# Row-wise infinity norm: two block sizes for the bulk rows and two stores instead of one

## The chip, the cores and the metric

The kernel runs on one core of a Trainium2 chip. The metric is the device time of one execution in microseconds (us); lower is better. Before the change three runs gave 626.51, 626.56 and 626.67 us, median 626.56.

## The reference

```python
x = np.random.randn(8192, 8192).astype(np.float32)   # 268 MB
out = np.linalg.norm(x, ord=np.inf, axis=1)           # per row
...
```

With `ord=np.inf` and `axis=1`, each row is a vector and its norm is the largest absolute value in it. So 8192 rows of 8192 floats (32 KB a row) are each reduced to one float. All of x has to be read once; the output is 32 KB.

## The kernel before, in words

The 8192 rows are spread over the 128 partitions, 64 rows to each. They come in two parts.

**Bulk.** The first 48 rows of each partition's share are read in A = 4 blocks. In one block, a partition owns G x B = 6 x 2 = 12 adjacent rows of HBM, so the places that two neighbouring partitions read from lie 12 rows (384 KB) apart. A block is read in six loads (line 303) of two rows a partition: 64 KB into each of the 128 partitions, 8.39 MB a load. After each load VectorE reduces it with one instruction, called at line 304 and recorded at line 296, to the absolute maximum of both rows, and writes two columns of the tile `r_bulk`. There are 24 such loads and 24 such reductions.

**Tail.** The last 16 rows of each partition's share are adjacent in HBM (512 KB from partition to partition). They are read in eight tiles of two rows as well, but each tile is cut into several loads of falling width (`TAIL`, lines 315 to 319, and `LAST`, lines 337 to 350), so that VectorE can start on each piece early. The partial maxima go to the tile `part`, or, for the last tile, beside its own data; the results go to `r_tail`. The narrow reductions of the last tile are the ones written `t<-t` in the profile.

**Queues and order.** All loads are issued by SP. There are three buffers `t`; a load into one waits until VectorE has reduced what was in it, so that SP is mostly two loads ahead of VectorE. The counters of DMA completion are used in turn; each is called a lane, DMAHW0 to DMAHW7 in the program's listing. ACT issues one store, that of `r_bulk` (line 357), ordered behind the last reduction but two of the last tile. The store of `r_tail` (line 359) is issued by SP after the last reduction. Five rewrites of the finished program (lines 360 to 364) then move the first load ahead of the opening barrier, drop waits that others imply, and let POOL close the program: it waits for the other open counters, clears the two ranges of counters on either side of the last store's lane, and finally waits for that last store (`finish_on_pool`).

Of the kernel before, what the change touches and what calls it, by code (L numbers as in the profile page):

```python
# [12 lines left out]
F32 = mybir.dt.float32  # L13
# [17 lines left out]
    + [(1, w) for w in (1664, 1408, 1280, 1152, 1024, 896)]  # L31
    + [(0, 768), (1, 768)]
)


HEAD, STEP = 32, 8


def segments(loads, cols):

    out, at = [], 0
    for i, w in enumerate(loads):
        end = at + w
        while at < end:
            r = at // cols
            to = min(end, (r + 1) * cols)
            out.append((i, r, at - r * cols, to - at))
            at = to
    return out
# [201 lines left out]
@with_exitstack  # L251
def kernel(
    ctx: ExitStack,
    tc: tile.TileContext,
    x: bass.AP,
    out: bass.AP,
    G: int = 6,
    B: int = 2,
    BUFS: int = 3,
    PAD: int = 256,  # L260
    LINE: int = 128,
):
    nc = tc.nc
    P = nc.NUM_PARTITIONS
    rows, cols = x.shape
    W = B * cols


    n_tail = B * (len(TAIL) + 1)
    n_bulk_rows = rows // P - n_tail  # L270
    assert n_bulk_rows % (G * B) == 0
    A = n_bulk_rows // (G * B)
    split = n_bulk_rows * P
    x_b = x[:split].rearrange("(a p n b) c -> a n p (b c)", p=P, a=A, n=G, b=B)
    out_b = out[:split].rearrange("(a p n b) -> p a (n b)", p=P, a=A, n=G, b=B)
    x_t = x[split:].rearrange("(p t b) c -> t p (b c)", p=P, b=B)
    out_t = out[split:].rearrange("(p t) -> p t", p=P)

    outp = ctx.enter_context(tc.tile_pool(name="outp", bufs=1))
    sbuf = ctx.enter_context(tc.tile_pool(name="sbuf", bufs=BUFS))  # L280

    segs = [segments(loads, cols) for loads in TAIL]
    k_max = max(sum(r == b for _, r, _, _ in s) for s in segs for b in range(B))
    parts_of = [sum(r == b for r, _ in LAST) - 1 for b in range(B)]
    assert sum(parts_of) <= PAD

    r_bulk = outp.tile([P, A, G * B], F32)
    r_tail = outp.tile([P, n_tail], F32)
    part = outp.tile([P, n_tail - B, k_max], F32)
    used = [HEAD, A * G * B, n_tail, (n_tail - B) * k_max]  # L290
    gap = -sum(-(-n // STEP) * STEP for n in used) % LINE
    outp.tile([P, gap], F32, name="gap")
    nc.gpsimd.memset(part[:], 0.0)  # L293

    def absmax(o, i):
        return nc.vector.reduce_max(  # L296
            out=o, in_=i, axis=X, apply_absolute_value=True
        )

    for a in range(A):  # L300
        for n in range(G):
            t = sbuf.tile([P, W + PAD], F32, tag="t")
            nc.sync.dma_start(out=t[:, :W], in_=x_b[a, n])
            absmax(
                r_bulk[:, a, n * B : (n + 1) * B],
                t[:, :W].rearrange("p (b c) -> p b c", b=B),
            )

    for i, loads in enumerate(TAIL):
        t = sbuf.tile([P, W + PAD], F32, tag="t")  # L310
        todo = segs[i]
        seen = [0] * B
        at = 0
        for j, w in enumerate(loads):
            nc.sync.dma_start(out=t[:, at : at + w], in_=x_t[i][:, at : at + w])
            at += w
            for _, b, c, n in [s for s in todo if s[0] == j]:
                k, lo = seen[b], b * cols + c
                absmax(part[:, i * B + b, k : k + 1], t[:, lo : lo + n])
                seen[b] += 1  # L320

    def after(ins, first, kind):
        info = mybir.DependencyInfo(kind, mybir.DependencyReason.SCHED_ONLY)
        tc.add_manual_dep(ins.ins, first.ins.name, info, reason="order")


    t = sbuf.tile([P, W + PAD], F32, tag="t")
    left = parts_of[:]
    col = [0] * B
    at, slot = 0, {}  # L330
    ends = [w for _, w in LAST[-B:]]
    lo = W - sum(ends)
    for b in range(B):
        slot[b] = -(-lo // LINE) * LINE + ends[b]
        lo = slot[b] + parts_of[b]
    assert lo <= W + PAD
    for j, (b, w) in enumerate(LAST):
        final = left[b] == 0
        to = slot[b] - w if final else at
        frm = b * cols + col[b]  # L340
        nc.sync.dma_start(out=t[:, to : to + w], in_=x_t[len(TAIL)][:, frm : frm + w])
        col[b] += w
        if final:
            r = n_tail - B + b
            absmax(r_tail[:, r : r + 1], t[:, to : slot[b] + parts_of[b]])
        else:
            left[b] -= 1
            k = slot[b] + left[b]
            done = absmax(t[:, k : k + 1], t[:, to : to + w])
            at += w  # L350
        if j == 0:

            ins = absmax(r_tail[:, : n_tail - B], part[:])
            after(ins, done, mybir.DependencyClass.NoSync)
        if j == len(LAST) - 3:

            ins = nc.scalar.dma_start(out=out_b, in_=r_bulk[:])
            after(ins, done, mybir.DependencyClass.Sync)
    nc.sync.dma_start(out=out_t, in_=r_tail[:])
    nc.at_finalize(clear_partials_early)  # L360
    nc.at_finalize(drop_implied_waits)
    nc.at_finalize(start_first_load_early)
    nc.at_finalize(finish_on_pool)
    nc.at_finalize(open_without_vector)
# [30 lines left out]
```

## Time and profile before

| What | Value |
|---|---|
| Median of three runs | 626.56 us |
| Span of the profiled execution (first to last recorded instruction) | 624.1 us |
| Time around the span, 626.56 - 624.1 | 2.5 us |
| DMA engines, mean rate over the span | 430 GB/s |
| One bulk load from issue to landing, median | 40.7 us |
| Bulk, first to last landing (21.76 to 466.68 us) | 444.92 us |
| Tail, last bulk landing to the start of the last pair of reductions | 154.79 us |
| Store of `r_bulk` from issue to landing | 2.4 us |
| Store of `r_tail` from issue to landing | 1.4 us |

The profiled execution is known by its span; its total time is not recorded apart from it, so the runs' median stands beside it. A line of instruction groups reads: line of the code, engine, operation, output and input tile with shapes, count, then the busy time in us, the mean of one in ns, and the idle time of the engine ahead of them with what ended it. A DMA issue's own length is the time that the issuing engine was occupied; the transfer goes on behind it until it lands. q1 is the queue of SP, q10 that of ACT.

### The profile page before, as it was taken

How to read it: one execution, taken by the hardware profiler on the slowest of the kernel's cores; microseconds unless marked ns; L12 is line 12 of the kernel's file. 1: busy time of each engine (PE TensorE's matmuls, PEld its weight loads, DVE VectorE, ACT ScalarE, POOL GpSimd, SP SyncE). 2: the span in 40 equal slices, each digit the busy share in tenths (PEclk: the TensorE clock that was granted, in tenths of full speed). 3: DMA queues.
4: the chain of work that ended last, by engine and by line, in shares of the span. 5: the costliest groups of instructions: out<-in, count | busy, mean ns of one | idle time of the engine just before them, and what ended most of it. 6: DMA issues, size and time to landing. Idle time of an engine off the chain costs nothing.

```text
span 624.1 us, 151 instructions
## 1 busy us (share of the span) xinstructions
DVE 552.4 (89%) x63; POOL 0.3 (0%) x5
## 2 busy tenths in 40 slices
DVE  0688988889988899888898888988889999999999
POOL 0000000000000000000000000000000000000000
DMA  9999999999999999999999999999999999999998
GB/s 403 470 403 454 420 428 445 403 470 403 470 403 441 433 403 470 403 470 403 470 403 470 403 462 412 437 437 403 470 434 397 440 448 422 422 437 430 429 427 354
DMA packets 8593, 268.47 MB, mean 430 GB/s; under 512 B 1424, under 2 KB 1424, under 8 KB 2832
## 3 DMA queue, kind: packets, MB, share of 16 engines
q1 hardware_dynamic: 8064, 268.44, 99.7%
q10 hardware_dynamic: 528, 0.02, 0.1%
q14 instruction: 1, 0.01, 0.0%
HBM read 268.44 MB, written 0.03 MB: 430 GB/s over the span
## 4 chain that ended last, share of the span: by engine, by line
DMA 63%; DVE 36%; another core or an unknown queue 0%; DVEq 0%; issue 0%
DMA t<-in_x_dram 63%; DVE r_bulk L296 25%; DVE part L296 8%; DVE t L296 3%; DVEq L390 0%; DVE r_tail L296 0%
## 5 line engine op out<-in xcount | busy, mean ns | idle before, releaser
L296 DVE TENSOR_REDUCE r_bulk<-t 128x2 f32<-128x16384 f32 x24 | 413.3, 17220 | 70.6 <-DMA t<-in_x_dram 70.6
L296 DVE TENSOR_REDUCE part<-t 128x1 f32<-128x8192 f32 (+19 forms) x26 | 121.3, 4741 | 0.3
L296 DVE TENSOR_REDUCE t<-t 128x1 f32<-128x1792 f32 (+7 forms) x10 | 16.3, 1692 | 0.0
L296 DVE TENSOR_REDUCE r_tail<-t 128x1 f32<-128x772 f32 (+1 forms) x2 | 1.8, 948 | 0.0
L296 DVE TENSOR_REDUCE r_tail<-part 128x14 f32<-128x42 f32 x1 | 0.2, 192 | 0.0
L293 POOL MEMSET part<- 128x42 f32 x1 | 0.1, 133 | 0.0
L379 POOL MEMSET const-bfloat16-1.0<- 128x1 bf16 x1 | 0.1, 101 | 0.0
L379 POOL MEMSET const-uint8-127<- 128x1 uint8 x1 | 0.1, 101 | 0.0
L379 POOL MEMSET const-float32-0.0<- 128x1 f32 x1 | 0.1, 98 | 0.2 <-issue 0.2
L379 POOL MEMSET const-float32-1.0<- 128x1 f32 x1 | 0.1, 98 | 0.0
## 6 DMA issues: line engine op xcount, KB each, us to landing
t<-in_x_dram SPq DMA_DIRECT2D x2, 4672.0 KB, 37.5
t<-in_x_dram SPq DMA_DIRECT2D x2, 3520.0 KB, 36.2
t<-in_x_dram SPq DMA_DIRECT2D x1, 6336.0 KB, 36.3
t<-in_x_dram SPq DMA_DIRECT2D x1, 5696.0 KB, 40.5
t<-in_x_dram SPq DMA_DIRECT2D x2, 1792.0 KB, 34.3
t<-in_x_dram SPq DMA_DIRECT2D x1, 3392.0 KB, 37.5
t<-in_x_dram SPq DMA_DIRECT2D x1, 3008.0 KB, 44.2
t<-in_x_dram SPq DMA_DIRECT2D x1, 2496.0 KB, 27.3
```

The lines of the kernel that those rows point to most:

```text
L293: nc.gpsimd.memset(part[:], 0.0)
L296: return nc.vector.reduce_max(out=o, in_=i, axis=X, apply_absolute_value=True)
L379: nc = _bacc.Bacc("TRN2", target_bir_lowering=False, num_devices=1)
```

## The change

The bulk's 48 rows a partition come no longer as four blocks of 12 adjacent rows, but as four blocks of 6 and then one block of 24. Each load still takes two adjacent rows from each partition's place, so there are 4 x 3 + 1 x 12 = 24 loads of the same size, and 24 reductions of the same shape, into the same columns. The result tile has 48 columns as before. Two neighbouring partitions' places lie 6 rows (192 KB) apart in the first four blocks and 24 rows (768 KB) in the last one.

As the two kinds of block leave their rows in two different patterns in the output, `r_bulk` is stored by two DMAs on ACT, one after the other, instead of one: 128 x 4 pieces of 6 floats (24 bytes), and 128 pieces of 24 floats (96 bytes). Before it was one of 128 x 4 pieces of 12 floats (48 bytes). The second store takes the next lane, DMAHW1, and waits for that lane's earlier load; the closing on POOL has one more counter to wait for.

```diff
+BLOCKS = [(4, 3), (1, 12)]
...
-    A = n_bulk_rows // (G * B)
-    split = n_bulk_rows * P
-    x_b = x[:split].rearrange("(a p n b) c -> a n p (b c)", p=P, a=A, n=G, b=B)
-    out_b = out[:split].rearrange("(a p n b) -> p a (n b)", p=P, a=A, n=G, b=B)
+    bulk, lo = [], 0
+    for a, g in BLOCKS:
+        hi = lo + a * g * B * P
+        bulk.append(
+            (
+                a,
+                g,
+                lo // P,
+                x[lo:hi].rearrange("(a p n b) c -> a n p (b c)", p=P, a=a, n=g, b=B),
+                out[lo:hi].rearrange("(a p m) -> p a m", p=P, a=a),
+            )
+        )
+        lo = hi
...
-    r_bulk = outp.tile([P, A, G * B], F32)
+    r_bulk = outp.tile([P, n_bulk], F32)
...
-    for a in range(A):
-        for n in range(G):
-            t = sbuf.tile([P, W + PAD], F32, tag="t")
-            nc.sync.dma_start(out=t[:, :W], in_=x_b[a, n])
-            absmax(
-                r_bulk[:, a, n * B : (n + 1) * B],
-                t[:, :W].rearrange("p (b c) -> p b c", b=B),
-            )
+    for a, g, col, x_b, _ in bulk:
+        for i in range(a):
+            for n in range(g):
+                t = sbuf.tile([P, W + PAD], F32, tag="t")
+                nc.sync.dma_start(out=t[:, :W], in_=x_b[i, n])
+                absmax(
+                    r_bulk[:, col : col + B],
+                    t[:, :W].rearrange("p (b c) -> p b c", b=B),
+                )
+                col += B
...
-            ins = nc.scalar.dma_start(out=out_b, in_=r_bulk[:])
-            after(ins, done, mybir.DependencyClass.Sync)
+            for a, g, c, _, out_b in bulk:
+                r = r_bulk[:, c : c + a * g * B]
+                ins = nc.scalar.dma_start(
+                    out=out_b, in_=r.rearrange("p (a m) -> p a m", a=a)
+                )
+                after(ins, done, mybir.DependencyClass.Sync)
```

More of the change, by code (lines that the diff above doesn't have):

```diff
@@ L256 @@
     out: bass.AP,
-    G: int = 6,
     B: int = 2,
@@ L269 @@
     n_tail = B * (len(TAIL) + 1)
-    n_bulk_rows = rows // P - n_tail
-    assert n_bulk_rows % (G * B) == 0
-    A = n_bulk_rows // (G * B)
-    split = n_bulk_rows * P
-    x_b = x[:split].rearrange("(a p n b) c -> a n p (b c)", p=P, a=A, n=G, b=B)
-    out_b = out[:split].rearrange("(a p n b) -> p a (n b)", p=P, a=A, n=G, b=B)
+    n_bulk = rows // P - n_tail
+    assert n_bulk == sum(a * g * B for a, g in BLOCKS)
+    split = n_bulk * P
+    bulk, lo = [], 0
[11 more added lines that the diff above has]
+        lo = hi
     x_t = x[split:].rearrange("(p t b) c -> t p (b c)", p=P, b=B)
@@ L285 @@
     assert sum(parts_of) <= PAD
-    r_bulk = outp.tile([P, A, G * B], F32)
+    r_bulk = outp.tile([P, n_bulk], F32)
     r_tail = outp.tile([P, n_tail], F32)
     part = outp.tile([P, n_tail - B, k_max], F32)
-    used = [HEAD, A * G * B, n_tail, (n_tail - B) * k_max]
+    used = [HEAD, n_bulk, n_tail, (n_tail - B) * k_max]
     gap = -sum(-(-n // STEP) * STEP for n in used) % LINE
```

## The prediction

> **What bounds the kernel now.** I read the page first, then the groups of instructions, the stretches, the timeline of VectorE and the DMA queues of the last microseconds. The page's busy shares and queue shares:
>
> ```profile
> DVE 552.4 (89%) x63; POOL 0.3 (0%) x5
> ...
> q1 hardware_dynamic: 8064, 268.44, 99.7%
> q10 hardware_dynamic: 528, 0.02, 0.1%
> ```
>
> The 16 DMA engines work on SP's loads (q1) for 99.7% of the span; VectorE, at 89%, has room. The groups say where that room is:
>
> ```profile
> L296 DVE TENSOR_REDUCE r_bulk<-t 128x2 f32<-128x16384 f32 x24 | 413.3, 17220 | 70.6 <-DMA t<-in_x_dram 70.6
> L296 DVE TENSOR_REDUCE part<-t 128x1 f32<-128x8192 f32 (+19 forms) x26 | 121.3, 4741 | 0.3
> ```
>
> All of VectorE's idle time of any size (70.6 us) stands before the 24 bulk reductions, and each time it ends with a load. So the bulk, the only part whose addresses the change touches, is bound by its loads. How evenly they come is seen in VectorE's timeline, where each start marks a landing (start, length, what, idle before it):
>
> ```profile
> 137.84 17.22 DVE L296 TENSOR_REDUCE r_bulk<-t 128x2 f32<-128x16384 f32 x1 [2.21 <-DMA t<-in_x_dram]
> 157.34 17.22 DVE L296 TENSOR_REDUCE r_bulk<-t 128x2 f32<-128x16384 f32 x1 [2.29 <-DMA t<-in_x_dram]
> ...
> 331.43 17.22 DVE L296 TENSOR_REDUCE r_bulk<-t 128x2 f32<-128x16384 f32 x1 [2.08 <-DMA t<-in_x_dram]
> 350.71 17.22 DVE L296 TENSOR_REDUCE r_bulk<-t 128x2 f32<-128x16384 f32 x1 [2.06 <-DMA t<-in_x_dram]
> ```
>
> The slowest gap between two landings is 157.34 - 137.84 = 19.50 us, the fastest 350.71 - 331.43 = 19.28 us. The stretches give the rate of the stages (stretch, length, VectorE, POOL, clock, DMA share, GB/s): the whole bulk from its first landing to its last, the tail, then those two gaps.
>
> ```profile
> 21.76:466.68 444.92, 396.05 (x23) 0.00 (x0) 1.00 1.00 433
> 466.68:621.47 154.79, 154.53 (x38) 0.00 (x0) 1.00 1.00 428
> 137.84:157.34 19.50, 17.22 (x1) 0.00 (x0) 1.00 1.00 430
> 331.43:350.71 19.28, 17.22 (x1) 0.00 (x0) 1.00 1.00 435
> ```
>
> The mean gap of the bulk is 444.92 / 23 = 19.34 us, 0.06 above the fastest one. In the tail DMA and VectorE are both full.
>
> **The time that the sum is made against.** The profiled execution is given by its span, 624.1 us; the runs' median is 626.56, so 2.5 us lie around the span. At least 0.6 of these come after it: the last store is issued at 623.31 and lands 1.4 us later, at 624.7. I assume the same 2.5 us after the change.
>
> **Part 1: the bulk's addresses.** Instructions, tiles, DMAs, waits and their order are the same on SP and VectorE: 24 loads of 128 x 16384 floats, still two adjacent rows (64 KB) from each partition's place, into the same buffers; 24 reductions of 17.22 us. What changes is the distance between partitions in HBM: 12 rows of 32 KB = 384 KB before, and now 6 rows = 192 KB for 24 rows a partition (12 loads) and 24 rows = 768 KB for the other 24 (12 loads). Nothing is added or removed, so only a different rate of the loads can pay or cost.
>
> What it can gain: if all 23 gaps became as short as the fastest, 444.92 - 23 x 19.28 = 1.5 us. No gap that is shorter stands in this trace, and the slow ones stand together: between the landings at 118.41 and 196.16 us four gaps in a row are 19.40 to 19.50, all of them in the second block, while the third and fourth blocks have gaps of 19.28 to 19.37 at the very same spacing. So the unevenness does not go by the spacing, and I expect none of the 1.5 us from it.
>
> What it can cost: the nearest rows are 384 KB (19.34 us a load) and the tail, whose partitions lie 16 rows = 512 KB apart: 155.6 us from the last bulk landing at 466.66 to the start of the last reduction at about 622.3, 8 x 8.39 MB, or 19.45 us for as much as one bulk load, with 32 smaller DMAs instead of 8. That is 0.11 more, and it includes the smaller sizes. If the 12 loads at 768 KB took that, it were 12 x 0.11 = 1.3 us. By the slowest gap, 0.16 above the mean, 12 loads cost 1.9 us and 24 cost 3.8. VectorE hides none of this: it idles 2.1 us a load and starts each reduction at the landing. I take zero, as 384 KB and the power of two 512 KB both stream with the DMA share at 1.00, and 768 is twice, 192 half of the spacing that the whole bulk has now.
>
> The Trainium skill speaks against such a change in "DMA: Bandwidth & Descriptors", section "Latency and other measured facts": copies whose rows lie large powers of two apart slow down, from 207 GB/s at 512 KiB to 164 at 2 MiB. The tail at 512 KB here agrees with the harmless end (428 GB/s); 192 and 768 KB are no powers of two and lie below 2 MiB, so by the rule as written I would add nothing, and no run here yet shows 768 KB. If 768 KB behaved as its 2 MiB row, an estimate from that page would be 12 x 19.3 x (207/164 - 1) = 61 us.
>
> **Part 2: one store becomes two.** The old bulk store moves 512 pieces of 48 bytes; now ACT issues one of 512 pieces of 24 bytes and a second of 128 pieces of 96. The end of the profile:
>
> ```profile
> 621.47 1.81 DVE L296 TENSOR_REDUCE r_tail<-t 128x1 f32<-128x772 f32 x2
> 621.59 0.41 ACTq L357 DMA_DIRECT2D out_dram<-r_bulk  x1
> 623.31 0.35 SPq L359 DMA_DIRECT2D out_dram<-r_tail  x1
> ```
> ```profile
> out_dram<-r_bulk ACTq DMA_DIRECT2D x1, 24.0 KB, 2.4
> out_dram<-r_tail SPq DMA_DIRECT2D x1, 8.0 KB, 1.4
> ```
>
> The second issue comes after the first, at 621.59 + 0.41 = 622.0, and takes 0.35 (r_tail's row) to 0.41, so ACT is free at about 622.4. Nothing is queued behind it but the end of the program, and that waits anyway for SP, which issues its last store at 623.31 to 623.66. The second store also waits for the lane (completion counter) DMAHW1 that it reuses: the load of 1408 columns, which landed before its reduction (1.61 us); the next one (1.48 us) ended where the last three before `r_tail` begin, at 618.10, so that load is some 5 us old by 621.59 and the wait costs nothing.
>
> Landing: the old store lands at 621.59 + 2.4 = 624.0. The second store's lower bound is r_tail's 1.4 us after its issue, 623.4; the upper bound is another 2.4, 624.4, if it queues fully behind the first. The queue's packets bear out less: q10 took 25.6% of 16 engines over 1.3 us for 528 packets, that is 0.256 x 1.3 x 16 / 528 = 0.010 us each. The 144 further packets (128 and 16 completions) are 9 an engine, 0.09 us. I take 624.1 for both. The cover is r_tail's store, which lands at 624.7: 0.6 us of room, 0.3 at the upper bound. From 623.2 to 624.1 no queue moves a packet in the trace, so the bulk store's packets are through 0.9 us before r_tail's begin, and 0.09 us more of them should not meet those.
>
> POOL closes the program after the other stores' counters and then r_tail's; one more wait is added, for the second bulk store. What POOL does between them isn't in the trace. If that work fills all the time after 624.0, a later bulk landing moves the end one for one: 0.1 us by my value, 0.4 at the upper bound. In the other direction two shorter stores could land earlier than one, but as r_tail's 624.7 stays, that gains at most a few hundredths.
>
> **Sum:** loads 0, reductions 0, stores 0 to 0.1: span 624.1, time 626.6 us.
>
> **The rivals.**
> - A, the stores come to the front: the second one lands at 624.4 and POOL's closing work is what ends last. 626.56 + 0.4 = 627.0. For it: two stores in one ring, and an unseen closing. Against it: 0.09 us by the packets. Still within 0.2%. It decides once the landing plus POOL's work passes 624.7.
> - B, slower: the block with 768 KB spacing streams less evenly in HBM, as in the slow gaps of this trace. At 0.16 us a load, 12 loads give 1.9 us: 628.5; if both new spacings do, 630.4. For it: gaps up to 19.50 exist, so something slows single loads. Against it: two different spacings run at full DMA share. It passes 0.2% (1.25 us) once each of the 12 loads takes 0.10 us more.
> - C, faster: the slow gaps were the old spacing's doing and all loads come at 19.28: 626.56 - 1.5 = 625.1. Against it: two of the four equal blocks already run without them.
> - D, the change doesn't do what it says: only addresses and one store differ, so there is nothing that a scheduler could undo; no chance of its own.
>
> **How the numbers follow.** Forecast 626.6 with 0.62; A 0.20; B 0.13; C 0.05. Forecast and A lie within 0.2%, which is about what a measurement of this kernel can tell from no change. Of C some 0.04 passes that bound, the full 1.5 us being needed nearly whole; of B some 0.12. So faster 0.04, same 0.84, slower 0.12. The range goes from 625.8 (half of C's gain) to 627.6 (A, and 0.05 us on each of 12 loads); B in full and C in full are left out.
>
> **What would show it.** Right: gaps between bulk landings of 19.3 us in both kinds of block, bulk stretch near 445 us; two ACT issues from 621.6 to 622.5; the second store landing before 624.7. B shows as gaps over 19.4 in the last 12 bulk loads alone, C as gaps of 19.28 all through, A as an unchanged span with a longer time, since POOL's close lies behind the span. I am wrong if the DMA share stays at 1.00 while a bulk stretch drops below 430 GB/s.

## The result and the profile after

The changed kernel takes 627.77 us (median of 20 runs, 627.39 to 628.16), the kernel before 626.57 (20 runs, 626.28 to 626.83): ratio 1.0019, 95% interval 1.0013 to 1.0026. It is slower by 1.2 us, just outside the range given. The profiled execution took 627.82 us, but its span is 624.0 us, no longer than the 624.1 of before. So 3.8 us lie around the span, where the table above has 2.5 for before. That 2.5 sets the runs' median against the span of another execution; taken within one execution, time minus span is 2.58 to 2.73 us in all 148 executions of the kernel before that were run beside the experiments (median 2.63), and 3.55 to 4.00 in the 20 of the changed kernel (median 3.82). So all of the 1.2 us lies around the span.

The page of the changed kernel shows the queues and VectorE as they were; q10 alone, the stores' queue, has 144 packets more:

```profile
DVE 552.4 (89%) x63; POOL 0.3 (0%) x5
...
q1 hardware_dynamic: 8064, 268.44, 99.7%
q10 hardware_dynamic: 672, 0.02, 0.1%
...
L308 DVE TENSOR_REDUCE r_bulk<-t 128x2 f32<-128x16384 f32 x24 | 413.3, 17220 | 70.6 <-DMA t<-in_x_dram 70.6
L308 DVE TENSOR_REDUCE part<-t 128x1 f32<-128x8192 f32 (+19 forms) x26 | 121.3, 4741 | 0.3
```

VectorE's idle time is 70.6 us again, all of it before the bulk's reductions. The timeline of VectorE in the changed kernel, at its longest and at one of its shortest gaps between landings:

```profile
234.67 17.22 DVE L308 TENSOR_REDUCE r_bulk<-t 128x2 f32<-128x16384 f32 x1 [2.15 <-DMA t<-in_x_dram]
254.13 17.22 DVE L308 TENSOR_REDUCE r_bulk<-t 128x2 f32<-128x16384 f32 x1 [2.24 <-DMA t<-in_x_dram]
...
331.39 17.22 DVE L308 TENSOR_REDUCE r_bulk<-t 128x2 f32<-128x16384 f32 x1 [2.08 <-DMA t<-in_x_dram]
350.67 17.22 DVE L308 TENSOR_REDUCE r_bulk<-t 128x2 f32<-128x16384 f32 x1 [2.06 <-DMA t<-in_x_dram]
```

The longest gap is 19.46 us, between the two kinds of block; that pair apart, the 192 KB loads take (234.67 - 22.03) / 11 = 19.33 us each, and the 768 KB loads (466.64 - 254.13) / 11 = 19.32. The stretches of the changed kernel (bulk from first to last landing, then the tail; columns as before) say the same:

```profile
22.03:466.64 444.61, 396.06 (x23) 0.00 (x0) 1.00 1.00 433
466.64:621.43 154.79, 154.53 (x38) 0.00 (x0) 1.00 1.00 428
```

444.61 us against 444.92, and the tail equal. The loss is in none of this. Now the end of the changed kernel, in its timeline and in its DMA issues (size of one in KB, median us from issue to landing):

```profile
621.43 1.81 DVE L308 TENSOR_REDUCE r_tail<-t 128x1 f32<-128x772 f32 x2
621.55 0.97 ACTq L373 DMA_DIRECT2D out_dram<-r_bulk  x2
623.27 0.35 SPq L377 DMA_DIRECT2D out_dram<-r_tail  x1
```
```profile
out_dram<-r_bulk ACTq DMA_DIRECT2D x2, 12.0 KB, 3.7
out_dram<-r_tail SPq DMA_DIRECT2D x1, 8.0 KB, 2.5
```

The issues come when they did before; the landings do not. The store of `r_tail`, unchanged and issued at 623.27, lands 2.5 us after its issue instead of 1.4: at 625.8 instead of 624.7, 1.1 us late. The tile's view of the output in the changed kernel has the three times to landing (3.9 is that of the first bulk store):

```profile
L373 ACTq DMA_DIRECT2D out_dram<-r_bulk x2: 412/464/517, 621.5 to 622.0; - x2
L377 SPq DMA_DIRECT2D out_dram<-r_tail x1: 348/348/348, 623.3 to 623.3; - x1
...
DMA to landing us min/median/max: 2.5/3.6/3.9
```

Read with the issue times, the bulk stores land 3.9 us after 621.55 and 3.6 after 622.00: at about 625.4 and 625.6, just ahead of `r_tail`'s 625.8. Were they still moving data? The DMA queues from 621.9 to 623.2 (40 slices of 0.03 us, then packets), before and then after:

```profile
DMA  0000000000000000080057998788768621110000
...
q10 hardware_dynamic: 528, 0.02, 25.6%
```
```profile
DMA  0000000000000000061356776677731011147553
...
q10 hardware_dynamic: 667, 0.02, 26.0%
```

Before, the last packets of the bulk store run at about 623.1, and it lands 0.9 us later, at 624.0. In the changed kernel 667 of q10's 672 packets start before 623.2, and the remaining five right behind, so the bulk stores' packets were through 2.2 us before the first landing. `r_tail`'s own packets are as early as before; the queues from 623.5 to 625.5 (slices of 0.05 us), before and then after:

```profile
DMA  0000000000000465200000000000000000000000
DMA  0000000000002653000000000000000000000000
```

They end near 624.4 both times, and `r_tail` lands 0.3 us later before and 1.4 us later after. What is late is not the transfer of either store but what comes between the last packet and the landing.

From that landing the end follows at a nearly fixed distance in every profiled run of this study, 1.9 to 2.0 us: 627.82 - 625.8 here; 626.57 (the median) - 624.7 before; 1.9 to 2.0 in all 18 experiments, each by the time of its profiled execution. So the time is the landing of the last store plus 2.0; what POOL does behind that landing takes the same time in every run.

### The profile page after: what moved, and what is told of

The parts are those of the page before. It is cut to its first block, busy times and chain, and to the rows that moved or that the text cites. A ratio compares the mean times of both kernels' runs of the same rounds, so it can differ in the third digit from the quotient of the medians.

```text
span 624.0 us, 152 instructions
## 1 busy us (share of the span) xinstructions
DVE 552.4 (89%) x63; POOL 0.3 (0%) x5
## 4 chain that ended last, share of the span: by engine, by line
DMA 63%; DVE 36%; another core or an unknown queue 0%; DVEq 0%; issue 0%
DMA t<-in_x_dram 63%; DVE r_bulk L308 25%; DVE part L308 8%; DVE t L308 3%; DVEq L408 0%; DVE r_tail L308 0%
## 5 line engine op out<-in xcount | busy, mean ns | idle before, releaser
L308 DVE TENSOR_REDUCE r_bulk<-t 128x2 f32<-128x16384 f32 x24 | 413.3, 17220 | 70.6 <-DMA t<-in_x_dram 70.6
```

The lines of the kernel that those rows point to most:

```text
L308: return nc.vector.reduce_max(out=o, in_=i, axis=X, apply_absolute_value=True)
```

## The experiments

Theory S: the bulk stores' completion is late, and the last store's waits behind it. Rival L blames the loads, rival N the mere second store with its waits. All times are medians, each compared with the kernel before on the same chip. With 8 to 11 runs the 95% interval of a ratio is about 0.0009 to either side, some 0.6 us. Two measures are finer: the landing of `r_tail` after its issue, which is known for one execution of each kernel, and the time around the span, which is known for all. "Around" in the tables is the median of time minus span in us; beside each experiment the kernel before has 2.60 to 2.65.

### Loads or stores, one store or two, 24 bytes or 96

**loads_only**: the changed loads, one store of 48-byte pieces.

```diff
-            for a, g, c, _, out_b in bulk:
...
+            out_b = out[:split].rearrange("(a p m) -> p a m", p=P, a=4)
+            ins = nc.scalar.dma_start(
+                out=out_b, in_=r_bulk[:].rearrange("p (a m) -> p a m", a=4)
+            )
...
```

> The loads of the change with the store of before: one DMA of 512 pieces of 48 bytes (so the bulk's results land in another order than the reference's). Theory S (the stores cost it: their confirmation is late and the last store's landing comes behind them): 626.5 to 626.7 us, r_tail's store landing 1.4 us after its issue, as before. Rival L (the loads cost it, outside what the span shows): 627.6 to 627.9.

**two48**: on the kernel before, its store cut in two.

```diff
-            ins = nc.scalar.dma_start(out=out_b, in_=r_bulk[:])
+            for a in (0, 2):
+                ins = nc.scalar.dma_start(
+                    out=out_b[:, a : a + 2], in_=r_bulk[:, a : a + 2]
+                )
...
```

> The loads of before; the store of before cut in two on ACT, 256 pieces of 48 bytes each. Theory S in the form 'small pieces' (24 bytes are confirmed late): 626.5 to 626.8, r_tail landing in about 1.4 us. Rival N (a second store in the queue, its wait or POOL's extra wait costs it): 627.4 to 627.9.

**only24** and **only96**: on the changed kernel, `bulk[:1]` or `bulk[1:]` in the loop of the stores.

> The changed kernel with its first store alone (512 pieces of 24 bytes); the store of the 24-row block, 96-byte pieces, is left out, so half of the bulk's results are not written. Small pieces: 627.5 to 627.9, the store landing 3 us or more after its issue and r_tail 2 us or more after its own. Rival N: 626.5 to 626.7.

> The changed kernel with its second store alone (128 pieces of 96 bytes); the store of the 6-row blocks, 24-byte pieces, is left out, so half of the bulk's results are not written. Small pieces: 626.4 to 626.7, the store landing in 2.4 us or less and r_tail in 1.4. If the 96-byte pieces are what is confirmed late: 627.4 or more. Rival N: 626.5 to 626.7.

| run | us | before | ratio (95%) | around | bulk store lands after | `r_tail` lands after |
|---|---|---|---|---|---|---|
| loads_only | 626.49 | 626.47 | 0.9999 (0.9990 to 1.0008) | 2.64 | 2.5 | 1.4 |
| two48 | 626.71 | 626.47 | 1.0003 (0.9994 to 1.0011) | 2.80 | 2.8 | 1.6 |
| only24 | 627.07 | 626.47 | 1.0009 (1.0000 to 1.0018) | 3.31 | 2.8 | 2.1 |
| only96 | 626.39 | 626.47 | 0.9998 (0.9989 to 1.0007) | 2.63 | 2.2 | 1.4 |

No cost of the loads is measured: rival L falls. With two stores of 48 bytes the medians differ by 0.24 us, which the interval does not tell from nothing; the time around the span is 0.17 longer and `r_tail` lands at 1.6, not at the expected 1.4. Rival N doesn't carry 1.2. The 24-byte store alone delays `r_tail` by 0.7 us and the time by 0.6, the expected sign at half the expected size; the 96-byte store alone costs nothing. Yet with the 96-byte store behind the 24-byte one, the delay is 1.1. The parts do not add up to the whole, 0.6 - 0.1 against 1.2.

One part of S failed in only24: its bulk store was expected to land 3 us or more after its issue and took 2.8. Timeline and DMA issues of only24:

```profile
621.37 0.41 ACTq L373 DMA_DIRECT2D out_dram<-r_bulk  x1
623.10 0.35 SPq L377 DMA_DIRECT2D out_dram<-r_tail  x1
...
out_dram<-r_bulk ACTq DMA_DIRECT2D x1, 12.0 KB, 2.8
out_dram<-r_tail SPq DMA_DIRECT2D x1, 8.0 KB, 2.1
```

The bulk store lands at 624.2, earlier than `r_tail` would with its usual 1.4 us (624.5), and `r_tail` still lands only at 625.2. So `r_tail`'s delay is not simply a wait for the bulk store's landing; the 24-byte store delays it by a way that the trace does not show.

### Is it the nearness in time to the last store?

**early**: the changed kernel with its bulk stores three reductions earlier.

```diff
-        if j == len(LAST) - 3:
+        if j == len(LAST) - 6:
```

> The changed kernel with both bulk stores issued three reductions of the last tile earlier, some 4 us, so that they are confirmed before the last store is issued. Theory S (the last store's confirmation waits behind the small pieces'): 626.3 to 626.7 us, r_tail landing 1.4 us after its issue again; the first bulk store itself still 3 us or more. Rival N (one more store and one more wait on POOL cost by themselves): 627.4 to 627.9. A small loss is possible from meeting the last loads: up to 0.1 us.

626.66 us, before 626.48, ratio 1.0005 (0.9996 to 1.0014). DMA issues of early:

```profile
out_dram<-r_bulk ACTq DMA_DIRECT2D x2, 12.0 KB, 5.7
out_dram<-r_tail SPq DMA_DIRECT2D x1, 8.0 KB, 1.6
```

The same two stores, the same counters for POOL, and nearly all of the loss is gone: 2.77 us around the span, and `r_tail` 0.2 us later than the expected 1.4. The bulk stores are even slower, 5.7 us, as they run between the last loads, but issued 3.6 us earlier (at 617.98) they land at 623.8 and 623.9, ahead of `r_tail`'s packets. So the loss needs the bulk stores close ahead of the last one, as S has it, and N falls.

### What makes the 24-byte pieces late

**rows16**: `BLOCKS = [(3, 8)]`, 384 pieces of 64 bytes.

> The bulk as three blocks of 16 adjacent rows: one store of 384 pieces of 64 bytes, each filling an aligned 64 bytes, and loads at 512 KB spacing. Small pieces: 626.2 to 626.6, the bulk store landing faster than the 2.4 us of 48-byte pieces, r_tail at 1.4. If the number of pieces decides and not their size, it lies with 48-byte pieces: 626.5.

**line24** and **dense24**: the changed loads, 384 pieces of 24 bytes; in line24 each has its own 64 bytes, in dense24 they lie end to end. The diff shows line24; dense24 writes the whole of `out[: 18 * P]`.

```diff
+            out_b = out[:split].rearrange("(a p m) -> p a m", p=P, a=3)
+            ins = nc.scalar.dma_start(
+                out=out_b[:, :, :6],
+                in_=r_bulk[:, :18].rearrange("p (a m) -> p a m", a=3),
+            )
```

> The changed kernel's loads and one store of 384 pieces of 24 bytes, each at the start of its own aligned 64 bytes (30 of the 48 columns are not stored, and what is stored lies elsewhere than in the reference). Theory P (a piece is late because it is only a part of what the memory writes at once): like only24 scaled to 384 pieces, 626.8 to 627.2, r_tail landing 1.8 us or later. Theory Q (it is late because neighbouring pieces write into the same 64 bytes): 626.4 to 626.6, r_tail at 1.4.

> The same 384 pieces of 24 bytes, but laid end to end as in the changed kernel (30 of the 48 columns are not stored). P and Q both: 626.8 to 627.2, r_tail landing 1.8 us or later; it is the control for line24, which differs in the addresses of the pieces alone.

rows16 takes 626.98 against 626.48, 1.0009 (0.9999 to 1.0018), above the expected 626.2 to 626.6: its store lands in 2.3 us and `r_tail` in 1.4 as expected, and 2.64 us lie around the span as before, but the span itself is longer (below). line24 takes 626.46 (1.0001; 0.9992 to 1.0010) and dense24 626.40 (0.9999; 0.9990 to 1.0008), both with `r_tail` at 1.4: 384 pieces delay nothing even end to end. The control, dense24, missed its expectation, so this pair decides nothing; the next one has more pieces.

**dense1024**, **room1024** and **line1024**: all 48 columns as 1024 pieces of 24 bytes, end to end in the output, end to end in a buffer of their own, and there with 64 bytes for each. The diff shows line1024; in room1024 the buffer has `8 * P * 6` floats and `out_b` is written whole, and in dense1024 `out[:split]` is.

```diff
+            room = nc.dram_tensor("room", (8 * P * 16,), F32, kind="Internal").ap()
+            out_b = room.rearrange("(a p m) -> p a m", p=P, a=8)
+            ins = nc.scalar.dma_start(
+                out=out_b[:, :, :6],
+                in_=r_bulk[:].rearrange("p (a m) -> p a m", a=8),
+            )
```

> The changed kernel's loads and one store of 1024 pieces of 24 bytes end to end (the results land in another order than the reference's). Theory W (the memory takes in 24-byte pieces at about 5.2 ns each, and the last store's completion comes behind what is left: 512 pieces from 622.32 kept r_tail waiting until 625.19, 384 did not): the backlog ends 1024 x 5.2 ns = 5.3 us after the first packet, near 627.7; r_tail lands 4.3 to 4.8 us after its issue, time 629.0 to 630.2. Rival F (a fixed delay that 24-byte stores draw when there are enough of them, not one that grows): 627.0 to 627.8.

> The same 1024 pieces of 24 bytes end to end, but in a buffer of their own in HBM instead of the output (the bulk's results are not stored in the output). Control for line1024: like dense1024, 629.0 to 630.2 under W, 627.0 to 627.8 under F. If it is quick, the place in memory decides: 626.4 to 626.7.

> The same 1024 pieces of 24 bytes in that buffer, each at the start of its own aligned 64 bytes (the bulk's results are not stored in the output). P (a piece is slow because it is smaller than what the memory writes at once): as room1024. Q (pieces are slow because neighbours go to the same 64 bytes): 626.4 to 627.2, r_tail landing 1.4 to 2 us after its issue.

| run | us | before | ratio (95%) | around | bulk store | `r_tail` |
|---|---|---|---|---|---|---|
| dense1024 | 627.63 | 626.46 | 1.0019 (1.0009 to 1.0028) | 3.73 | 3.8 | 2.5 |
| room1024 | 627.88 | 626.46 | 1.0024 (1.0014 to 1.0034) | 3.92 | 3.9 | 2.7 |
| line1024 | 626.49 | 626.46 | 1.0000 (0.9991 to 1.0009) | 2.62 | 2.8 | 1.4 |

DMA issues of room1024, then of line1024:

```profile
room<-r_bulk ACTq DMA_DIRECT2D x1, 24.0 KB, 3.9
out_dram<-r_tail SPq DMA_DIRECT2D x1, 8.0 KB, 2.7
```
```profile
room<-r_bulk ACTq DMA_DIRECT2D x1, 24.0 KB, 2.8
out_dram<-r_tail SPq DMA_DIRECT2D x1, 8.0 KB, 1.4
```

The same 1024 packets of 24 bytes on the same queue; only their addresses differ, and the whole loss comes and goes with them. So the size and the number of the pieces (P, or the DMA's work on them) do not make the loss by themselves; that they lie end to end (Q) does. Number still counts, as dense24 shows. The same pair shows that `r_tail` is late although the bulk goes into another buffer and on another queue. Theory W failed: it expected 629.0 to 630.2, and the two dense runs took 627.63 and 627.88, the one within rival F's 627.0 to 627.8 and the other 0.1 above.

### What of lying end to end

Two explanations are left: two pieces write into one unit of memory, or a piece crosses the boundary between two units. The bulk's results go into a buffer of their own again, as 1024 pieces in each run. What shares and what crosses is worked out on the assumption that the buffer begins on a multiple of 64 bytes; no view gives its address.

**half1024**: `8 * P * 8` floats, a piece at every 32 bytes. **strad1024**: `8 * P * 32` floats and `out_b[:, :, 13:19]`.

> 1024 pieces of 24 bytes in the buffer of their own, at every 32 bytes: two pieces share 64 bytes, no piece crosses a boundary of 32 (the bulk's results are not stored in the output). Sharing of 64 bytes (theory Q): 627.2 to 628, r_tail landing 2 us or later. Crossing: 626.4 to 626.6, r_tail at 1.4. If what must not be shared is 32 bytes, also 626.4 to 626.6; strad1024 then tells the two apart.

> 1024 pieces of 24 bytes, one in every 128 bytes, starting 52 bytes in, so that each crosses a boundary of 64 bytes and none shares its 64 bytes with another (the bulk's results are not stored in the output). Sharing: 626.4 to 626.6, r_tail at 1.4. Crossing: 627.2 to 628, r_tail landing 2 us or later.

**share16** and **own16**: four of each six columns, in a buffer of `8 * P * 4` floats written whole, or of `8 * P * 8` with `out_b[:, :, :4]`.

> 1024 pieces of 16 bytes end to end in the buffer of their own: two pieces share each aligned 32 bytes, none crosses a boundary (the bulk's results are not stored in the output, and two of each six columns are left out). If sharing 32 bytes is what makes end-to-end pieces slow: 627.2 to 628, r_tail landing 2 us or later. If it takes a shared unit and a crossing together, as in 24-byte pieces: 626.4 to 626.7, r_tail at 1.4 to 1.6.

> The same 1024 pieces of 16 bytes at every 32 bytes: nothing is shared below 64 bytes and nothing crosses (what is left out is as in share16). Sharing of 32 bytes: 626.4 to 626.6, r_tail at 1.4, as half1024. If pieces of 16 bytes are slow for their size: with share16.

| run | same 64 bytes | same 32 bytes | crosses | us | before | ratio (95%) | around | bulk store | `r_tail` |
|---|---|---|---|---|---|---|---|---|---|
| half1024 | yes | no | no | 626.59 | 626.42 | 1.0004 (0.9995 to 1.0014) | 2.65 | 2.9 | 1.4 |
| strad1024 | no | no | yes | 626.55 | 626.42 | 1.0002 (0.9993 to 1.0011) | 2.72 | 3.1 | 1.6 |
| own16 | yes | no | no | 626.58 | 626.39 | 1.0002 (0.9992 to 1.0012) | 2.67 | 2.8 | 1.4 |
| share16 | yes | yes | no | 627.01 | 626.39 | 1.0010 (1.0000 to 1.0020) | 3.25 | 3.5 | 2.0 |
| room1024 | yes | yes | yes | 627.88 | 626.46 | 1.0024 (1.0014 to 1.0034) | 3.92 | 3.9 | 2.7 |

DMA issues of share16, then of own16:

```profile
room<-r_bulk ACTq DMA_DIRECT2D x1, 16.0 KB, 3.5
out_dram<-r_tail SPq DMA_DIRECT2D x1, 8.0 KB, 2.0
```
```profile
room<-r_bulk ACTq DMA_DIRECT2D x1, 16.0 KB, 2.8
out_dram<-r_tail SPq DMA_DIRECT2D x1, 8.0 KB, 1.4
```

Sharing 64 bytes does next to nothing. Sharing an aligned 32 bytes delays `r_tail` by 0.6 us with no crossing at all; crossing without sharing by 0.2 in its one trace and by 0.1 around the span; both together by 1.3. The time of share16 lies at the edge of its interval and below the 627.2 that was expected, but its 3.25 us around the span, against 2.60 of the kernel before beside it, tell the same as its landing.

Sharing alone is not the whole of it. The 512 pieces of 48 bytes end to end, as in the store of before, share 32 bytes too, one place for every two pieces or 256 in all, and loads_only loses nothing (counted on the same assumption); dense24 shares 288 and loses nothing. only24 shares 384 (0.7 us), share16 512 (0.6), dense1024 and room1024 768 (1.1 and 1.3). So few shared places were free, and how the delay depends on their number was not worked out.

**after_lines**: the changed kernel's two stores, 24-byte pieces in 64 bytes each and 96-byte pieces in 128 each, into two buffers.

> The changed kernel with its two stores as they are in count and size, but each 24-byte piece at the start of its own 64 bytes and each 96-byte piece at the start of its own 128, in buffers of their own (the bulk's results are not stored in the output). If end-to-end pieces are the whole loss: 626.4 to 626.7, r_tail at 1.4. If a second store adds a part of its own, as in two48 (0.24): 626.7 to 627.

626.45 us against 626.42, ratio 1.0001 (0.9992 to 1.0010). DMA issues of after_lines:

```profile
room<-r_bulk ACTq DMA_DIRECT2D x2, 12.0 KB, 2.4
out_dram<-r_tail SPq DMA_DIRECT2D x1, 8.0 KB, 1.4
```

With the change's loads, both its stores, their sizes and POOL's wait all in place, and only the addresses pulled apart, the loss is gone: 2.65 us lie around the span, against 2.62 of the kernel before beside it and 3.82 of the changed kernel. The buffers differ from the output as well, but room1024, in such a buffer, loses no less than dense1024. So the addresses of the pieces account for the 1.2 us.

### Other block sizes

**rows48**: `BLOCKS = [(1, 24)]`. **rows24**: `BLOCKS = [(2, 12)]`.

> The bulk as one block of 48 adjacent rows, 1536 KB from partition to partition: one store of 128 pieces of 192 bytes, each three aligned 64 bytes. By W the backlog is gone long before the last store: 626.2 to 626.5, the best of all if the loads at that spacing keep 19.34 us. If the first load starts later, as it did in rows16 (first landing 22.40 against 21.76): up to 627.2.

> The bulk as two blocks of 24 adjacent rows: all loads at 768 KB spacing, one store of 256 pieces of 96 bytes end to end. If that spacing costs nothing, as loads_only said of 12 such loads: 626.3 to 626.6, first landing before 22.0 us. If the first load is late at wide spacings, as in rows16 and rows48: 626.9 to 627.1, first landing at 22.3 or later, the rest of the loads even.

rows24 takes 626.59 against 626.42, 1.0003 (0.9995 to 1.0012), first landing at 21.99; the 768 KB spacing is harmless by this one too. rows48 takes 627.02 against 626.46, 1.0008 (0.9999 to 1.0016). Its stores are as good as hoped, `r_tail` at 1.4, but the first landing is late. Timeline of rows48:

```profile
22.50 17.22 DVE L308 TENSOR_REDUCE r_bulk<-t 128x2 f32<-128x16384 f32 x1 [22.50 <-DMA t<-in_x_dram]
```

22.50 us here and 22.40 in rows16, against 21.76 before. after_lines started as late in its profile (22.42) and lost nothing over its runs, so a single first landing proves little. The spans of all runs say where the 0.5 us lie: their median is 624.4 us in rows48 and 624.3 in rows16, against 623.8 of the kernel before, and 2.64 us lie around them as before. So they lie within the span and not in what follows the last store; their cause was not tried. No experiment points to a version that beats the kernel before: in none did `r_tail` land sooner than 1.4 us after its issue, as there.

## Why the prediction was wrong

- **Loads, zero: right.** The gaps are 19.33 and 19.32 us; loads_only measures the whole of Part 1 at 0.02 us. Rivals B and C did not occur, and no load slowed down at 768 KB.
- **Issue of the second store, its lane's wait: right.** Issued at 622.0; ACT was free by 621.55 + 0.97 = 622.5. It took 0.52 rather than 0.35 to 0.41, under cover. The lane's earlier load was older than the 5 us given, some 621.59 - 618.10 + 1.48 + 1.61 = 6.6, which changes nothing.
- **Landing of the bulk stores, "I take 624.1 for both": wrong, and this is the step that failed.** They landed at 625.4 and 625.6, beyond the upper bound of 624.4. I priced the second store by its packets, "9 an engine, 0.09 us". The packets were indeed cheap: they ended near 623.2 as forecast. But the store of before already took some 0.9 us from its last packet, at about 623.1, to its landing at 624.0, and this piece I never priced. In the changed kernel it was 2.2 us. It depends on how the pieces lie in HBM: 512 pieces of 24 bytes end to end share their 32 bytes with neighbours, and the same pieces apart cost nothing (after_lines; line1024 for 1024).
- **"As r_tail's 624.7 stays": wrong, and with it the cover.** I let the two stores meet only if their packets met. They met behind their packets: `r_tail` landed 1.1 us late, and the end 1.2 us. The Trainium skill states in "DMA: Bandwidth & Descriptors", section "Queues, rings and completion order", that the write which raises a DMA's counter lands only after every earlier write of that DMA engine, across its queues. The traces agree in the order: `r_tail` landed last in every profiled run, and in room1024 it was 1.3 us late behind ACT's store into another buffer. They do not show that this order is what delays it, as in only24 `r_tail` landed 1.0 us after the bulk store had. What should have warned me was in the trace of before: the bulk store's 0.9 us behind its last packet, where `r_tail` has 0.3.
- **Rival A: the right place, the wrong mechanism and size.** It had the stores come to the front, by 0.4 us through POOL's closing. What POOL does at the close was fixed: the end came 1.9 to 2.0 us after `r_tail`'s landing in every profiled run. It forecast an unchanged span with a longer time, and that was seen.
- **The 2.5 us around the span: taken as fixed, and wrong.** Within one execution it is 2.63 before and 3.82 after, and the whole loss sits there.
- **The size**: the change moved the time by 0.19%, inside the 0.2% given 0.84, but to 627.77 where the range ended at 627.6. That it stayed inside the 0.2% is luck, as no term of the sum had this loss. The range's upper end came from A and the loads; a bound on the unpriced completion was missing.

Open: how the delay grows with the number of pieces (none at 384, 0.7 us at 512, 1.1 to 1.3 at 1024), why the harmless 96-byte store behind the 24-byte one raised the delay from 0.7 to 1.1, and what holds `r_tail` back in only24 after the bulk store has landed. That sharing 32 bytes costs was measured; what the memory does about it was not seen.

## What to carry to other kernels

A store at the end of a kernel is priced by its landing, not by its packets: here stores issued 1.7 us before the last one delayed its landing by up to 1.3 us, from another queue, into another buffer too, and after their own packets had gone. When a layout is changed, look at the pieces that it writes to HBM as well as at those it reads: pieces of 64, 96 and 192 bytes were free here, and so were pieces of 16 and 24 bytes with 32 bytes to each; 512 or more pieces of 24 bytes and 1024 of 16 bytes end to end were not. A small store that must have bad pieces goes out some microseconds earlier; 3.6 us took the loss from 1.2 to 0.2 us.

## What the hardware showed that I had not expected

- 1024 packets of 24 bytes land in 2.8 us with 64 bytes to each and in 3.9 end to end; a spacing of 32 bytes suffices (2.9).
- A store issued on SP landed up to 1.3 us later because of a store on ACT whose packets had all gone when its own began (room1024).
- 192, 384 and 768 KB between partitions read at the same 19.3 us a load of 8.39 MB, with the DMA share at 1.00.
